# Order of the input projection beside the attention: the first output-gate unit third, six convolution units behind it

## The chip, the cores and the metric

The kernel runs on one core of a Trainium2 chip. The metric is the device time of one execution in microseconds; the time given is the median of several executions. The core's engines work side by side, each through its own list of instructions in order: TensorE (PE in the profile; its weight loads are PEld), VectorE (DVE), ScalarE (ACT), GpSimd (POOL) and SyncE (SP), which issues most DMAs.

## What is computed

One layer of an encoder on a sequence of 1024 tokens of width 1024, in float32. One input projection feeds two groups of heads; what they give is concatenated and projected back, and a SwiGLU network follows.

```python
h = modulate(rms_norm(x, norm_mix_g[l]), sh1, sc1)
proj = h @ w_in[l]
q_a, k_a, v_a, qk_m, v_m, o_m, gates = jnp.split(proj, splits, axis=-1)
y_attn = axial_gqa_attention(q_a, k_a, v_a, q_norm_g[l], k_norm_g[l], tables)
y_mem = bidirectional_mlstm(qk_m, v_m, o_m, gates, conv_w[l], conv_b[l], gate_b[l], mlstm_norm_g[l])
mix = jnp.concatenate([y_attn, y_mem], axis=-1) @ w_out[l]
x = x + g1[:, None, :] * mix
```

The attention has 8 query heads of 64 on 2 key heads, with rotary positions and a softmax over all 1024 keys. The mLSTM has 4 heads of 128 and runs over the sequence in both directions. Its queries and keys, `qk_m`, are 1024 columns that go through a convolution along the sequence, five taps wide, and a silu. Its values `v_m` and its output gates `o_m` are 512 columns each. Input gates and forget gates are 16 columns, of which running sums and maxima are taken.

## The kernel before

Each float32 product is made of three matmuls (`mm3`, lines 310 to 313): both operands are split into a high and a low part, and high by high, high by low and low by high are summed. The normed input lies in SBUF for the whole first half of the program as `hh` and `hl` (8 tiles of 128 rows each).

**The input projection is cut into units.** Those named `q` make two query heads each (`q_unit`). Those named `f` make 128 channels of the convolution's input each (`conv_unit`, line 878): `f` 0 to 3 are the mLSTM's queries, 4 to 7 its keys. Those named `t` make 256 columns, turned so that tokens lie on the partitions (`chunk_unit`, line 936): `t` 0 and 1 are the values of mLSTM heads 0 and 1, and 2 and 3; `t` 2 and 3 the output gates of the same pairs. The list `IN` (lines 47 and 48) is the order in which the units that are left after the program's first stage are gone through.

A conv unit is two halves of 512 tokens, each a sum over 8 steps of three matmuls of 512 columns into a PSUM bank named `acc`. ScalarE copies each half into the tile `xp`. Then a chain of steps follows: five taps on VectorE into the tile `y` (one `TENSOR_SCALAR`, four `SCALAR_TENSOR_TENSOR` of 128x1024), a tanh on ScalarE, a last product on VectorE, and a store to DRAM. A chunk unit is eight parts of 128 tokens, each a sum over 8 steps of three matmuls of 256 columns into a bank named `acct`; ScalarE copies each part into the tile `vstg`, and SP stores it. In the attention's stage `acc` and `acct` share one single bank.

A conv unit begins by waiting for the chain of the conv unit two before it:

```python
yield convs[-2:-1]
```

Weights come in pieces of 256 KB, in the order in which the units use them (`specs`, which is built from `IN` too). A conv unit has two pieces, a chunk unit four. A piece is loaded by SP into the tile `wst`, copied by ScalarE to `whi` and subtracted by GpSimd to `wlo`. There is room for six split pieces. A unit calls for further pieces as it goes through the last of its own (`load_piece`, line 487): a conv unit in its second half, a chunk unit in its last part.

**The order of instructions comes from a planner.** While the program is built, `Clock` keeps an estimated time for every engine. `streams` (line 215) takes the streams in their order of rank: at each step of PE the first stream whose operands are ready by that clock goes on, and the `fills` come last. On the chip every engine goes through the order so found, and waits by semaphores where the estimate was too early.

```python
s = next((s for s in every if s.ready() <= self.t), None)
```

**The attention** is made of three streams of higher rank than the units, over 64 blocks of 128 queries of one head each. `scores` (line 1146) makes the score product `S`; VectorE takes its maximum (`sst`), ScalarE the exponential (`P`, with its sum), VectorE the reciprocal, and GpSimd scales `P`. `turned` (line 1178) transposes `P` on PE into `T`; ScalarE and VectorE copy it out as high and low part (`PT`). `values` (line 1200) multiplies with the values into `av`. Every eight blocks a new head's queries are split (`qs`, ScalarE and GpSimd). Beside them run, on GpSimd and ScalarE, the products for the conditioning (`ada`, `ada_late`, line 1111), and on VectorE and ScalarE the gates' steps (`gate_steps`, line 954; running sums and maxima in the tiles `Fr`, `T`, `mk`, `R`, one step no sooner than 10 us after the other by the planner's clock, line 69). The units are the fill:

```python
ck.streams([Stream(values()), Stream(turned()), Stream(scores())], [un])
ck.streams([un], stop=lambda: convs[-1].done and len(convs) == 8 and not open_sum[0])
```

Units that are left when the attention ends, and when all eight convolutions are done, go on as the fill beside the mLSTM (line 2191), and the output projection's units after them.

Of the kernel before, what the change touches and what calls it, by code (L numbers as in the profile page):

```python
# [43 lines left out]
KB = 5  # L44
AHEAD = 2
NP = NF // 2
IN = ([("q", 2), ("q", 3), ("f", 0), ("f", 4), ("f", 1), ("f", 5), ("t", 2), ("f", 2), ("f", 6),
       ("f", 3), ("f", 7), ("t", 1), ("t", 3)])
MIX = [("o", i) for i in range(16)] + [("m", (i + 8) % 16) for i in range(16)]
FF = [("b", p) for p in range(NB)] + [("v", 0)] + [("s", (p, i)) for p in range(1, NP - 1) for i in range(2)] + [("v", NP - 1)]  # L50
# [199 lines left out]
def layer_kernel(ctx, tc, xT, c, w_ada, vecs, cons, rope, w_f, w_fT, w_t0, w_t, w_o, w_gu, w_d, out):  # L250
# [113 lines left out]
    with tc.manual_schedule():  # L364
# [65 lines left out]
        specs += [t0[0], q1[0], t0[1], t0[2], q1[1], t0[3]]  # L430
        for kind, i in IN + MIX + FF:
            start[kind, i] = len(specs)
# [1656 lines left out]
        def units(order):  # L2089
            for kind, i in order:  # L2090
                yield from {"q": q_unit, "f": conv_unit, "t": chunk_unit, "o": out_unit, "m": out_unit, "b": first_unit, "s": set_unit, "v": pair_unit}[kind](i, start[kind, i])
# [56 lines left out]

        un = Stream(units(IN))
        def ready():  # L2150
            return rope_ok[3].done and logf_ok.done and not open_sum[0]
# [162 lines left out]
```

## Time and profile before

| | us |
|---|---|
| median of 3 runs (1390.51 to 1393.83) | 1393.42 |
| the profiled execution | 1393.51 |
| its span, from the first to the last instruction | 1391.7 |
| first score product | 174.3 |
| end of the attention's last product | 505.1 |

The units' places in the profiled execution, read off the copies of their sums by ScalarE:

| unit | last copy starts at, us |
|---|---|
| f0 | 156.3 |
| f4 | 178.2 |
| f1 | 207.2 |
| f5 | 244.5 |
| t2 | 327.9 |
| f2 | 352.3 |
| f6 | 373.1 |
| f3 | 403.6 |
| f7 | 431.0 |

In rows of the profile a group is written as line, engine, operation, `out<-in` by the tiles' names, and partitions by elements. Line 98 is the helper through which VectorE, ScalarE and GpSimd get all their instructions, so these are told apart by their tiles. Lines 311 to 313 are the three matmuls of `mm3`, line 1158 is `S`, 1190 `T`, 1209 `av`. A row of the timeline begins with its start in us and its length; in brackets stands how long the engine was idle before it, and what ended the idle time. A row of the table by stage gives the stage, its length, the busy time and the number of instructions of each engine, then the granted clock of TensorE as a share of full speed, the DMA engines' share and GB/s.

### The profile page before, as it was taken

To read this page: it belongs to the slowest core of one execution; us is meant where nothing else is said; L and a number is where in the kernel's file an instruction comes from. 1 tells how busy PE (TensorE), PEld (TensorE's weight loads), DVE (VectorE), ACT (ScalarE), POOL (GpSimd) and SP (SyncE) were. 2 spreads that over 40 slices of the span, in tenths; PEclk is the share of its full clock that TensorE was granted. 3 is DMA by queue.
4 is the path that set the end of the run, shared out by engine and by line. 5 is a ranking of instruction groups with operands and counts; after the bars stand their busy time and mean duration, and the time that the engine had idled before them with its cause. 6 is when DMAs were issued, how large, how long until landed. Compare 5 with 4: busy or idle time off the path is not lost.

```text
span 1391.7 us, 19566 instructions
## 1 busy us (share of the span) xinstructions
PE 1289.2 (93%) x6588; PEld 1079.7 (78%) x6596; DVE 1033.3 (74%) x1536; ACT 709.0 (51%) x1335; POOL 706.1 (51%) x584
## 2 busy tenths in 40 slices
PE   7898888899999979989997899999999999979997
PEld 5786677888778978777776788888888887857887
DVE  6936698975789747758689886766676654998866
ACT  6575366778577755454477333332333334344462
POOL 0344677655656525677512265554554545445542
PEclk9999999999999999999999899999999999989999
DMA  9444433233233235663652343233332259733324
GB/s 355 158 129 118 114 103 95 84 99 105 65 108 97 67 131 180 201 225 102 198 187 89 105 138 106 99 107 106 114 114 81 76 178 328 288 79 103 95 64 155
DMA packets 103892, 185.98 MB, mean 134 GB/s; under 512 B 11504, under 2 KB 33136, under 8 KB 103792
## 3 DMA queue, kind: packets, MB, share of 16 engines
q1 hardware_dynamic: 90400, 162.63, 36.8%
q10 hardware_dynamic: 13392, 22.10, 4.2%
q8 instruction: 52, 0.85, 0.2%
q14 instruction: 48, 0.39, 0.1%
HBM read 137.76 MB, written 43.25 MB: 130 GB/s over the span
## 4 chain that ended last, share of the span: by engine, by line
PE 55%; DVE 18%; issue 8%; DMA 6%; ACT 5%; POOL 5%; SPq 1%; DVEq 0%; POOLq 0%; ACTq 0%
PE acc L311 15%; PE acc L312 15%; PE acc L313 15%; DVE sst L98 3%; DVE y L98 2%; DVE PT L98 2%; PE av L1209 2%; DVE x L98 2%; PE T L1190 2%; POOL wlo L98 2%; PE S L1158 1%; SPq L316 1%; DMA x<-in_xT_dram 1%; PE acct L313 1%; DVE s L98 1%
## 5 line engine op out<-in xcount | busy, mean ns | idle before, releaser
L98 POOL TENSOR_TENSOR wlo<-wst,whi 128x512 fp32r<-128x512 f32 (+2 forms) x187 | 264.5, 1420 | 262.3 <-ACT whi L98 236.4
L98 ACT ACTIVATE whi<-wst 128x512 fp32r<-128x512 f32 (+2 forms) x219 | 131.0, 605 | 110.2 <-PE acc L313 34.2
L312 PE MATMUL acc<-x,whi 128*128 128x512 f32 x352 | 138.4, 393 | 5.9 <-DVE x L98 5.9
L98 POOL TENSOR_SCALAR P<-P,sst 128x1024 f32<-128x1024 f32 x64 | 85.1, 1330 | 88.1 <-DVE sst L98 64.3
L98 POOL TENSOR_TENSOR wlo<-wr,whi 128x512 fp32r<-128x512 f32 x56 | 77.4, 1383 | 76.9 <-ACT whi L98 75.5
L311 PE MATMUL acc<-hh,whi 128*128 128x512 f32 x224 | 97.8, 436 | 6.5 <-ACT xp L98 5.3
L311 PE MATMUL acc<-whi,wch 128*128 128x512 f32 x244 | 96.5, 395 | 6.1 <-ACT wch L98 6.1
L313 PE MATMUL acc<-whi,wcl 128*128 128x512 f32 x244 | 96.8, 397 | 2.9 <-DVE wcl L98 2.8
L312 PE MATMUL acc<-wlo,wch 128*128 128x512 f32 x244 | 96.1, 394 | 0.1
L98 ACT ACTIVATE P<-S,sst,colq 128x1024 f32<-128x1024 f32 x64 | 77.2, 1207 | 36.8 <-DVE sst L98 26.9
L98 ACT ACTIVATE whi<-wr 128x512 fp32r<-128x512 f32 x60 | 37.9, 632 | 107.5 <-DVE wr L98 50.1
L98 DVE TENSOR_TENSOR PT<-T,PT 128x512 fp32r<-128x512 f32 x128 | 83.3, 681 | 10.7 <-ACT PT L98 10.5
L312 PE MATMUL acc<-hl,whi 128*128 128x512 f32 x224 | 90.9, 406 | 0.0
L313 PE MATMUL acc<-hh,wlo 128*128 128x512 f32 x224 | 90.8, 405 | 0.0
L98 POOL TENSOR_TENSOR wlo<-s,whi 128x512 fp32r<-128x512 f32 x40 | 54.0, 1352 | 67.5 <-ACT whi L98 67.5
L1190 PE MATMUL T<-ident,P 128*128 128x128 f32 x512 | 72.8, 280 | 15.9 <-DVE PT L98 9.3
L98 DVE TENSOR_TENSOR sg<-acc,sg 128x512 f32<-128x512 f32 x67 | 45.4, 687 | 55.8 <-PE acc L313 55.5
L311 PE MATMUL acct<-whi,hh 128*128 128x256 f32 (+1 forms) x256 | 82.8, 324 | 4.2 <-ACT hh L98 2.8
L98 ACT ACTIVATE PT<-T 128x512 fp32r<-128x512 f32 x128 | 71.8, 596 | 28.5 <-PE T L1190 27.8
L98 DVE TENSOR_REDUCE sst<-S 128x1 f32<-128x1024 f32 x64 | 77.7, 1214 | 11.4 <-PE S L1158 9.9
L312 PEld LDWEIGHTS acc<-x,whi 128*128 128x128 f32 x352 | 66.5, 189 | 21.0 <-DVE x L98 7.3
L98 POOL TENSOR_TENSOR ada<-ada,cond 128x512 f32<-128x512 f32 x48 | 69.2, 1443 | 23.3 <-DMA ada<-in_w_ada_dram 23.2
(478 smaller groups left out, 3859.6 us busy)
## 6 DMA issues: line engine op xcount, KB each, us to landing
wr<-in_w_gu_dram SPq DMA_DIRECT2D x66, 256.0 KB, 2.7
ada<-in_w_ada_dram SPq DMA_DIRECT2D x64, 256.0 KB, 3.2
wd<-in_w_d_dram SPq DMA_DIRECT2D x22, 512.0 KB, 6.4
wst<-in_w_gu_dram SPq DMA_DIRECT2D x34, 256.0 KB, 3.1
wst<-act_d SPq DMA_DIRECT2D x33, 256.0 KB, 4.1
ada<-in_w_ada_dram SPq DMA_DIRECT2D x16, 512.0 KB, 7.1
wst<-in_w_o_dram SPq DMA_DIRECT2D x32, 256.0 KB, 3.9
act_d<-sg ACTq DMA_DIRECT2D x31, 256.0 KB, 2.2
```

Source lines behind the costliest of these rows:

```text
L98: return fn(*args, **kw)
L311: nc.tensor.matmul(acc, w[0], x[0], start=first, stop=False)
L312: nc.tensor.matmul(acc, w[0], x[1], start=False, stop=False)
L313: nc.tensor.matmul(acc, w[1], x[0], start=False, stop=last)
L316: (q or nc.sync).dma_start(dst, src)
L1158: nc.tensor.matmul(sp[:, halves(n)], qs[:, j * P:(j + 1) * P], k2[g][m][:, halves(n)], start=m == 0, stop=m == 1)
L1190: nc.tensor.transpose(tp[:, k], Pt[q][:, (4 * b + k) * P:(4 * b + k + 1) * P], ident)
L1209: nc.tensor.matmul(av, va[:, k, h // 4], PT[it][m][:, k], start=(k, m) == (0, 0), stop=(k, m) == (NJ - 1, 1))
```

## The change

The unit `t` 2 moves from the seventh place of `IN` to the fifth, ahead of `f` 1 and `f` 5. Among the units behind the two of queries it is now third, and the six conv units left follow it without a break. The weight pieces follow, since their list is built from `IN`. The instructions are otherwise the same; their order on every engine is the planner's.

```diff
-IN = ([("q", 2), ("q", 3), ("f", 0), ("f", 4), ("f", 1), ("f", 5), ("t", 2), ("f", 2), ("f", 6),
+IN = ([("q", 2), ("q", 3), ("f", 0), ("f", 4), ("t", 2), ("f", 1), ("f", 5), ("f", 2), ("f", 6),
        ("f", 3), ("f", 7), ("t", 1), ("t", 3)])
```

## The prediction

> **What bounds the kernel now.** I read the page first, then the table by stage, then the chain of work, then the timelines at the places where TensorE stood idle. From the page:
>
> ```profile
> PE 1289.2 (93%) x6588; PEld 1079.7 (78%) x6596; DVE 1033.3 (74%) x1536; ACT 709.0 (51%) x1335; POOL 706.1 (51%) x584
> PE 55%; DVE 18%; issue 8%; DMA 6%; ACT 5%; POOL 5%; SPq 1%; DVEq 0%; POOLq 0%; ACTq 0%
> ```
>
> TensorE (PE) is busy 93% of the span and carries 55% of the chain that ended last, so the program is nearly a list of matmuls, and time is won only where PE idles or runs at a lower clock. The change adds and removes no instruction. It can only move that idle time. The attention runs from its first score product at 174.3 us to 505.1 us, and the table by stage (length, then busy time of PE, PEld, DVE, ACT, POOL; the granted clock follows) cuts it where the fill changes its kind:
>
> ```profile
> 174.30:196.40 22.10, 18.27 (x91) 14.83 (x90) 20.32 (x24) 12.89 (x24) 18.46 (x14) 0.92 0.32 96
> 196.40:244.80 48.40, 42.83 (x235) 36.25 (x234) 42.71 (x59) 31.90 (x63) 34.41 (x22) 0.93 0.33 98
> 244.80:281.30 36.50, 31.87 (x234) 29.17 (x233) 35.69 (x53) 25.60 (x52) 24.13 (x17) 1.00 0.28 84
> 281.30:328.30 47.00, 43.60 (x322) 40.21 (x320) 34.41 (x62) 39.50 (x83) 27.19 (x24) 1.00 0.37 108
> 328.30:432.70 104.40, 98.63 (x558) 82.74 (x559) 79.17 (x131) 69.12 (x136) 60.04 (x50) 0.98 0.30 91
> 432.70:505.10 72.40, 68.71 (x518) 64.10 (x516) 56.85 (x99) 53.74 (x106) 37.38 (x27) 1.00 0.21 62
> ```
>
> PE idles 3.83, 5.57, 4.63, 3.40, 5.77 and 3.69 us in them, 26.9 us in all. DVE is the second engine to fill up: 92%, 88%, 98%, 73%, 76%, 79%.
>
> Which fill runs where, by the same table for one tile's instructions: first acc (conv units, one row), then acct (units of 256 columns, one row), then y (the convolutions' taps; the first number is DVE's, three rows):
>
> ```profile
> 328.30:432.70 104.40, 55.09 (x192) 34.17 (x192) 0.00 (x0) 4.76 (x8) 0.98 0.30 91
> ...
> 281.30:328.30 47.00, 18.76 (x114) 15.93 (x114) 0.00 (x0) 1.93 (x5) 1.00 0.37 108
> ...
> 196.40:244.80 48.40, 12.11 (x8) 2.12 (x2) 0.93 0.33 98
> 244.80:281.30 36.50, 10.03 (x6) 1.06 (x1) 1.00 0.28 84
> 281.30:328.30 47.00, 0.00 (x0) 0.00 (x0) 1.00 0.37 108
> ```
>
> A conv unit is 48 matmuls, so the 192 at 328.3 to 432.7 are exactly the four units f2, f6, f3, f7. The two stretches before that are t2, the unit that moves; those from 174.3 to 244.8 are the end of f4, then f1 and f5. The taps trail their unit: f5's fall into t2's first half, and t2's second half has none.
>
> **The change part by part.** Until f4 is through (its last half runs across the start of the attention) both orders are the same. Then f1, f5, t2 become t2, f1, f5. Loads: t2 has four weight pieces, f1 and f5 two each, all of 256 KB, so the list of pieces keeps its shape, and the same numbers of loads stand on SP's queue, ACT and POOL. SP's stores (8 small ones of t2, one of 512 KB for each conv) swap places among themselves; nothing in the attention reads them, so I put that at nothing. If it were not hidden, one late store would hold a buffer for a few microseconds. From f2 on the order is the old one.
>
> *What goes.* The two largest waits in f1 and f5 (PE's timeline, S is L1158, T is L1190; in brackets the idle time before and who ended it):
>
> ```profile
> 215.21 1.07 PE L1158 MATMUL S<-k,qs 128*128 128x512 f32 x4
> ...
> 219.12 0.66 PE L1190 MATMUL T<-ident,P 128*128 128x128 f32 x4 [2.16 <-POOL P L98]
> ...
> 222.47 1.65 PE L1158 MATMUL S<-k,qs 128*128 128x512 f32 x4
> ...
> 232.86 0.63 PE L1190 MATMUL T<-ident,P 128*128 128x128 f32 x4 [2.95 <-POOL P L98]
> ```
>
> Both wait for POOL to scale a softmax block. After the first the same score products take 1.65 us for 1.07: the clock has dropped. The clock column says how much: 0.93 over 48.4 us is 3.4 us lost, and 0.92 over 22.1 us is 1.8 us. Why POOL was late (POOL's timeline, then DVE's):
>
> ```profile
> 213.40 2.35 POOL L98 TENSOR_TENSOR ada<-ada,cond 128x512 f32<-128x512 f32 x1 [2.04 <-DMA ada<-in_w_ada_dram]
> 215.71 2.25 POOL L98 TENSOR_TENSOR wlo<-wst,whi 128x512 fp32r<-128x512 f32 x1
> 217.96 1.11 POOL L98 TENSOR_SCALAR P<-P,sst 128x1024 f32<-128x1024 f32 x1
> ...
> 226.19 4.51 POOL L98 TENSOR_TENSOR qs<-qd,qs 64x1024 fp32r<-64x1024 f32 x1
> 230.80 1.97 POOL L98 TENSOR_SCALAR P<-P,sst 128x1024 f32<-128x1024 f32 x1
> ...
> 226.21 2.27 DVE L98 TENSOR_TENSOR_SCAN Fr<-mk,Fr 32x1024 f32<-32x1024 f32 x1
> 228.46 3.32 DVE L98 SCALAR_TENSOR_TENSOR y<-xp,vec,y 128x1024 f32<-128x1024 f32 x1
> ```
>
> Three loads meet here: weight splits (wlo), gate scans, and f1's taps; the P step takes 1.97 us instead of 1.11, and a tap 3.32 us. With t2 in this place, f1's taps are not yet there (12.11 us of DVE work in the stretch, of which only f4's last step stays), and no weight split comes until t2's end. The gate scans stay: they are paced on their own.
>
> *The sum*, over 174.3 to 328.3. Before: idle 3.83 + 5.57 + 4.63 + 3.40 = 17.4, clock 1.8 + 3.4 = 5.2, together 22.6 us.
>
> After: (a) to 196.4, f4's taps still meet the first scan: 3.8 + 1.8 = 5.6, as now. (b) t2 took 83 us; some 64 us of it now lie behind 196.4, with scans but no taps. The nearest row is t2's tapless half, 3.40 of 47.0, or 7.2%: 4.6 us, no clock lost. (c) f1 and f5 come in some 67 us. For the first 36.5 us f1's taps meet the remaining gate steps, as f5's do now at 244.8 to 281.3: 4.6 us. (d) The other 30 us resemble the run of four conv units: 5.77 idle and 0.02 of clock in 104.4, 7.5%: 2.3 us. Together 17.1 us. **The gain is 22.6 - 17.1 = 5.5 us.** Bounds: at best t2 also takes away (a)'s clock loss and its 1.9 us wait, and (c) falls to the rate of (d), another 5 us; at worst f1 and f5 keep all of their old waits (5.57 + 3.4 = 9.0 instead of the 6.9 in c and d) and t2 its own 8.0, and nothing is won.
>
> The profiled execution took 1393.51 us with a span of 1391.7, beside a median of 1393.42, so the sum holds for both: 1393.5 - 5.5 = **1388.0 us**. Work that no longer fits into a shorter attention (the rest of t1, all of t3) goes on beside the mLSTM, at no less cost and no more: it is PE work in either place.
>
> The Trainium skill, "TensorE: Matmul & The Clock Gate", "What's actually happening", has the array's clock halve after an idle window of about 3.4 us; by that neither wait above would cost clock, and the estimated gain would be about 2 us. The trace differs: 1.65 us for 1.07 stands behind a wait of 2.16 us.
>
> **The rivals.** *The pile-up travels.* Taps and POOL's steps lengthen each other, and the taps only move. For it: the taps meet P, ada and weight splits wherever they run, and in 281.3 to 328.3, where f5's taps would then fall, ACT is 84% busy (39.50 of 47.0) against 66% where f1's taps lie now (31.90 of 48.4). Against it: the four conv units from 328.3 on have the same taps and lose 7.5% of their time, where f1 and f5 lose 18.5% (5.57 + 3.4 of 48.4). Price: f1 and f5 keep 9.0 us and t2 keeps 8.0, which is what they lose now: 1393 us, give or take 3. The Trainium skill, "SBUF — State Buffer", "Who interferes with whom", speaks for this rival: a VectorE instruction with two SBUF inputs and a GpSimd instruction that reads SBUF hold a shared port in turn, each for its whole length. The 3.32 us tap agrees.
>
> *Slower: a conv unit waits for the chain of the one two before it* (line 879). Six in a row means that f2 cannot start until f1's taps, tanh, product and store are done, and f6 not until f5's are. The chain's and the passes' lengths (evacuations on ACT, last product on DVE):
>
> ```profile
> 244.47 0.60 ACT L98 ACTIVATE xp<-acc 128x512 f32<-128x512 f32 x1
> ...
> 352.27 0.60 ACT L98 ACTIVATE xp<-acc 128x512 f32<-128x512 f32 x1
> ...
> 373.14 0.60 ACT L98 ACTIVATE xp<-acc 128x512 f32<-128x512 f32 x1 [5.72 <-PE acc L313]
> ...
> 279.12 1.86 DVE L98 SCALAR_TENSOR_TENSOR y<-xp,y 128x1024 f32<-128x1024 f32 x1
> ...
> 388.60 1.22 DVE L98 SCALAR_TENSOR_TENSOR y<-xp,y 128x1024 f32<-128x1024 f32 x1
> ```
>
> f5's chain beside the gate steps takes 36.5 us (244.47 to 280.98), f6's only 16.7 (373.14 to 389.82); f6's pass on PE takes 20.9 (352.27 to 373.14), and four passes 104.4, or 26.1 each. Today t2 stands behind f5 and hides the long chain. If f1's and f5's chains both take 36.5 us, f2 and f6 wait 10.4 each, 20.8 us in which PE has no fill. The fill is 55.09 of 104.4 there, 53%, so at most 11.0 us of PE time is lost, plus two drops of the clock like those above (3.4): 1388.0 + 14.4 = 1402; at the least the attention speeds up without fill and half is lost: 1395. I take 1398. It decides from about 10 us of waiting on (5.5 / 0.53). Against it: only f1 will meet the gate steps, f5 just the last of them.
>
> **How the numbers follow.** A measurement of this kernel can tell 0.3%, 4.2 us, from no change. The forecast, 1383 to 1391, has a chance of 0.5; the travelling pile-up 0.3; the hold of the conv chains 0.2. Of the forecast some 0.06 lies within 4.2 us of before, and of the travelling pile-up some 0.02 on either side: faster 0.46, same 0.32, slower 0.22. The range takes the best bound of the sum (1388.0 - 5) and reaches up to the middle of the slower rival: 1382.5 to 1398.5.
>
> **What would show it.** Right: the waits of T for P near 219 and 233 are gone, the clock from 196 to 245 is 1.00, no y instruction starts on DVE between about 203 and 260, and the last tap still comes some 50 us ahead of the attention's end, which has moved from 505.1 to about 499.6. The travelling pile-up would show as waits of T for P or PT of over 2 us between 265 and 330, with a clock under 1.00. The slower rival would show as stretches without any acc matmul near 310 or 335, while PE idles. What would make the prediction wrong besides: the order of all instructions comes from a planner's clock, which may place the gate steps elsewhere once DVE is freer, against other work than I assumed.

## The result, and the profile after

The changed kernel takes 1414.28 us (median; 1413.9 to 1416.05) beside 1393.14 us of the kernel before on the same chip: a ratio of 1.0167, 95% interval 1.0149 to 1.0184. It is 21 us slower, where 5.5 us less had been forecast. The page's first two lines of the profiled execution:

```profile
span 1412.8 us, 19571 instructions
PE 1287.6 (91%) x6596; PEld 1077.8 (76%) x6596; DVE 1044.6 (74%) x1536; ACT 705.9 (50%) x1335; POOL 700.1 (50%) x584
```

PE is busy as long as before (1287.6 us for 1289.2), so the 21 us are idle time. The question is in which stage. The table by stage of the changed kernel, cut at the attention's first and last product and at the mLSTM's last transpose of an output (in the kernel before, the attention's last product ends at 504.2; 505.1 is where the next product starts):

```profile
175.00:513.70 338.70, 310.73 (x2036) 274.05 (x2035) 273.25 (x421) 233.69 (x465) 201.15 (x152) 0.99 0.29 90
513.70:690.70 177.00, 138.03 (x772) 117.07 (x772) 120.84 (x271) 78.50 (x205) 103.65 (x144) 0.90 0.51 164
690.70:1412.80 722.10, 689.81 (x3108) 567.13 (x3106) 535.11 (x667) 294.67 (x501) 324.05 (x238) 0.98 0.40 133
```

The same three stages of the kernel before:

```profile
174.30:504.20 329.90, 303.92 (x1950) 267.31 (x1948) 268.70 (x421) 232.37 (x458) 201.62 (x150) 0.98 0.30 88
504.20:671.40 167.20, 146.68 (x849) 124.81 (x857) 117.24 (x271) 82.11 (x212) 109.26 (x147) 0.98 0.55 182
671.40:1391.70 720.30, 688.90 (x3108) 566.68 (x3106) 531.51 (x667) 295.53 (x501) 326.10 (x240) 0.98 0.40 134
```

The attention is 8.8 us longer (338.7 for 329.9), the mLSTM's stage 9.8 (177.0 for 167.2), the rest 1.8; the start is 0.7 later. But the two stages differ in kind. The attention's extra time is filled: PE idles 28.0 us in it for 26.0 before, and executes 84 more matmuls (the row counts two more, which begin just before the cut and belong to the next stage). In the mLSTM's stage PE executes 77 matmuls fewer and still takes longer: it idles 39.0 us for 20.5.

Those matmuls are fill. The same table for the tile acct (units of 256 columns), attention and mLSTM's stage, of the changed kernel:

```profile
175.00:513.70 338.70, 70.62 (x446) 61.19 (x447) 0.00 (x0) 6.84 (x18) 0.99 0.29 90
513.70:690.70 177.00, 17.62 (x132) 16.17 (x131) 0.00 (x0) 2.31 (x6) 0.90 0.51 164
```

And of the kernel before:

```profile
174.30:504.20 329.90, 60.40 (x360) 50.50 (x360) 0.00 (x0) 5.72 (x15) 0.98 0.30 88
504.20:671.40 167.20, 34.54 (x216) 29.12 (x216) 0.00 (x0) 3.44 (x9) 0.98 0.55 182
```

With three matmuls to a step, and without the two at the cut, the attention took in 148 steps of t units for 120. The 28 steps are worth some 10.1 us of PE time (an estimate: three matmuls 0.12 us apart are 0.36 us). On equal work, then, the attention became some 1.3 us shorter, and the mLSTM's stage, which should have become 10.1 us shorter, lost 19.9. What PE waited for in that stage (who waited for whom; total, times, longest):

```profile
PE U L1910 <- DVE Cs L98: 20.9, 1, 20.9
...
PE acc L311 <- ACT yah L98: 6.2, 1, 6.2
```

One wait of 20.9 us, at 539 to 560. DVE's step Cs, for which it waits, stands in DVE's list behind this (the chain that ended last, in order of time: start, length, what):

```profile
540.24 3.47 DMA ada<-in_w_ada_dram
...
543.80 1.19 DVE ada L98 x2
545.01 2.37 DMA ada<-in_w_ada_dram
...
547.48 0.71 DVE ada L98 x2
548.21 3.00 DMA ada<-in_w_ada_dram
...
558.62 0.70 DVE ada L98 x2
```

Load, product, load, product: the late pieces of the conditioning (ada) come two at a time, a pair each 3.7 us (543.80 to 558.62 in four), and nothing else is put out. The code says why. The mLSTM's first stage lasts until the projection's units are through; then whatever ada pieces are left are gone through alone, because their memory is wanted for the next stage:

```python
ck.streams(mem, [un], stop=lambda: un.wait is None and all(f.done for v in vo_ok for f in v))
while not summed:
    ck.need(*adas[-2:])
    ada_late(64)
```

In the kernel before, t3 runs until 577 us, and all ada pieces are done by then (the last product starts at 557.8). In the changed kernel t3 is through at 537 us. ScalarE's copies of the t units' sums, before and after (shortest, median and longest in ns, then the first and the last start in us):

```profile
L98 ACT ACTIVATE vstg<-acct x32: 369/384/403, 84.1 to 577.5; 128x256 f32<-128x256 f32 x32
L98 ACT ACTIVATE vstg<-acct x32: 367/384/404, 82.5 to 537.3; 128x256 f32<-128x256 f32 x32
```

**Theory A**: the time is lost because the attention used up t3's steps, so the stage ended with ada pieces undone. **Theory B**, the rival: the run of six conv units, or the early place of t2, costs the time.

### The profile page after: what moved, and what is told of

It is laid out like the page before. It is cut to its first block, busy times and chain, and to the rows that moved or that the text cites. A ratio compares the mean times of both kernels' runs of the same rounds, so it can differ in the third digit from the quotient of the medians.

```text
span 1412.8 us, 19571 instructions
## 1 busy us (share of the span) xinstructions
PE 1287.6 (91%) x6596; PEld 1077.8 (76%) x6596; DVE 1044.6 (74%) x1536; ACT 705.9 (50%) x1335; POOL 700.1 (50%) x584
## 4 chain that ended last, share of the span: by engine, by line
PE 55%; DVE 21%; issue 8%; ACT 6%; DMA 5%; POOL 3%; SPq 1%; DVEq 0%; ACTq 0%; POOLq 0%
PE acc L312 15%; PE acc L313 15%; PE acc L311 15%; DVE sst L98 4%; DVE y L98 3%; DVE PT L98 3%; PE av L1209 2%; DVE x L98 2%; PE T L1190 1%; DMA ada<-in_w_ada_dram 1%; PE S L1158 1%; ACT P L98 1%; SPq L316 1%; DVE s L98 1%; PE ni L1994 1%
## 5 line engine op out<-in xcount | busy, mean ns | idle before, releaser
L98 DVE TENSOR_TENSOR PT<-T,PT 128x512 fp32r<-128x512 f32 x128 | 83.8, 681 | 14.4 <-ACT PT L98 14.3
L1209 PE MATMUL av<-PT,va 128*128 128x256 f32 x512 | 73.9, 288 | 11.6 <-DVE PT L98 9.9
```

Source lines behind the costliest of these rows:

```text
L98: return fn(*args, **kw)
L1209: nc.tensor.matmul(av, va[:, k, h // 4], PT[it][m][:, k], start=(k, m) == (0, 0), stop=(k, m) == (NJ - 1, 1))
```

## The experiments

Each run is measured against the kernel before on the same chip.

**1. The changed kernel with the stage held open.** One condition more:

```diff
-ck.streams(mem, [un], stop=lambda: un.wait is None and all(f.done for v in vo_ok for f in v))
+ck.streams(mem, [un], stop=lambda: un.wait is None and all(f.done for v in vo_ok for f in v) and summed)
```

> The changed kernel, with one condition more: the mLSTM's first stage, whose fill is what is left of the projection's units, ends only when the conditioning products (ada) are done too, so that they run beside mLSTM steps instead of by themselves. Theory A (the time is lost because t3 is used up early, the stage ends, and 10 of the 16 ada pieces are then waited for with no other work put out; PE idle for 20.9 us at 539 to 560 in the changed kernel): the idle stretch goes, some 5 us of it come back as unfilled gaps of the mLSTM, 1395 to 1402. Theory B (the run of six conv units, or t2's early place, costs the time inside the attention): 1408 to 1414, since the attention is the same. A third reading, that the 20.9 us would only be passed on to the next stage: 1410 or more, with an idle stretch later.

Measured: 1396.07 us, ratio 1.004 (1.002 to 1.006). Its mLSTM's stage, by the same table:

```profile
512.10:672.50 160.40, 138.40 (x759) 115.35 (x766) 114.74 (x270) 78.47 (x204) 104.41 (x142) 0.96 0.54 178
```

160.4 us for 177.0, with an attention as long as in the changed kernel (337.6 us). Its largest wait in that stage is 2.4 us. One condition on a stage's end brings back 1.3% of the 1.7%: theory A, and not B. What the 0.4% left is made of was not tried.

**2. The old order with its fill used up.** All units left are run at the attention's end:

```diff
-ck.streams([un], stop=lambda: convs[-1].done and len(convs) == 8 and not open_sum[0])
+ck.streams([un])
```

> The kernel before, its old order of units, with one edit: behind the attention all units that are left run at once, so that the mLSTM starts without any fill and its first stage ends at once, with all 16 ada pieces (32 halves, 16 behind the attention) still to come. Theory A: an idle stretch of PE of 25 to 35 us while they come alone, 1415 to 1430. Theory B: the old order has no run of six, so the time stays within 1393 to 1400.

Measured: 1444.86 us, ratio 1.0399 (1.0363 to 1.0436). The wait appears in the old order too:

```profile
PE tr L1882 <- issue: 37.7, 1, 37.7
```

It is longer than expected, but not by the ada pieces. The chain that ended last, inside this wait (which begins at 535.5):

```profile
538.05 4.48 DMA cond<-in_c_dram
...
545.06 2.38 DVE ada L98 x4
547.46 2.55 DMA ada<-in_w_ada_dram
...
570.17 0.71 DVE ada L98 x2
```

The 16 pieces take 25.8 us (545.06 to 570.88), at the low end of the 25 to 35 expected; the 9.5 us ahead of them go mostly to a store and to the conditioning's own input (cond), which here nothing hides either. The time is 15 us above the range: the whole mLSTM then runs without t3, and PE idles 66.7 us up to its end, of which the wait is only 37.7. The direction is A's; the price of a missing fill was set too low.

**3. t2 one place later than before.** No run of six conv units:

```diff
-IN = ([("q", 2), ("q", 3), ("f", 0), ("f", 4), ("f", 1), ("f", 5), ("t", 2), ("f", 2), ("f", 6),
+IN = ([("q", 2), ("q", 3), ("f", 0), ("f", 4), ("f", 1), ("f", 5), ("f", 2), ("t", 2), ("f", 6),
        ("f", 3), ("f", 7), ("t", 1), ("t", 3)])
```

> The order of before with t2 one place later, behind f2: runs of conv units of five and three, none of six, and t2 in the middle of the attention. Theory A: what matters is how much fill the attention takes in, and if this order also takes in more, t3 is used up early here too; by the same idle stretch, 1408 to 1418. Theory B: the shorter runs and the later place put it beside the kernel before, 1388 to 1398.

Measured: 1414.97 us, ratio 1.0192 (1.0151 to 1.0233), the same loss as the changed kernel's. (This kernel has one line less ahead of the code, so its line numbers are one lower.)

```profile
PE U L1909 <- DVE Cs L97: 20.5, 1, 20.5
```

The same wait to half a microsecond, with t2 on the other side of its old place, and again 148 steps of t units in the attention. This speaks most plainly against B: neither the long run of conv units nor the early place is needed for the loss.

**4. The changed order with t3 kept out of the attention.**

```diff
-un = Stream(units(IN))
+un = Stream(units(IN[:-1]))
...
-ck.streams([un], stop=lambda: convs[-1].done and len(convs) == 8 and not open_sum[0])
+ck.streams([un])
+un = Stream(units(IN[-1:]))
```

What is left of t1 is now run before the mLSTM starts; in the trace the attention takes in all of it.

> The changed order, but t3 is kept out of the attention's fill: it starts only with the mLSTM. Theory A: the mLSTM's first stage then has 64 steps of fill (some 23 us of PE time) and lasts until the ada pieces are nearly done; the idle stretch shrinks to under 3 us and the attention loses some fill at its end: 1393 to 1402. Theory B: 1408 to 1414, since the conv units run as in the changed kernel.

Measured: 1391.97 us, ratio 1.0018 (1.0 to 1.0036); in a second series beside the next run 1391.52, ratio 1.0009 (0.9995 to 1.0024), where this stood on record:

> The same kernel as in the earlier run of the changed order with t3 kept back, again, beside the old order with the same edit on one chip: ratio to the kernel before 0.999 to 1.005. By the prediction's sum it would lie 5.5 us under the old order with the edit, by theory B over 4 us above it, and if the attention's idle time only moves, within 3 us of it.

The mLSTM's stage of the first series:

```profile
510.90:668.30 157.40, 141.89 (x824) 120.75 (x833) 119.26 (x271) 79.18 (x207) 103.52 (x143) 0.99 0.57 185
```

157.4 us for 177.0, idle 15.5 for 39.0. With the fill at the place where it is needed, the changed order is level with the kernel before.

**5. The old order with the same edit.**

> The order of before with the edit of the run before (t3 starts only with the mLSTM). In the kernel before the stage's end already finds the ada pieces done, so under theory A the edit changes little: 1386 to 1396 (ratio 0.998 to 1.004). Its ratio against the changed order with the same edit is then what the order alone does to the attention: the prediction's sum has 5.5 us less for the changed order, theory B has over 4 us more, and that the idle time only moves gives under 3 us either way.

Measured: 1398.53 us, ratio 1.0062 (1.0045 to 1.0079), above the range. With this edit the changed order is 7 us ahead of the old one. That looks like the 5.5 us of the prediction, and is not: the attention of this run is as in the kernel before (329.4 us, PE idle 27.3), and the difference lies in the mLSTM's stage (176.2 us for 157.7 in the second series of the changed order). There PE waits twice at the end:

```profile
PE ni L1994 <- DVE num L98: 6.7, 2, 5.9
PE acc L311 <- ACT yah L98: 5.3, 1, 5.3
```

The second is the wait of 6.2 us of the changed kernel: the output projection's second half waits for the mLSTM's last heads, when its first half, the next fill, is used up. Why the old order uses it up here and the changed one does not stays open: this fill starts at 560.4 in the one and at 558.4 in the other. Nor does the attention show a gain for the changed order: it takes 337.0 us there (PE idle 30.3), 7.6 more than in this run, for 8 more steps of fill (some 2.9 us), which the old order runs behind the attention. So this pair does not isolate the order's effect on the attention, as it was meant to.

**6. ada pieces earlier, in the old order.** The attention's blocks may take pieces beyond the 48th:

```diff
-                ada_late()
+                ada_late(64)
```

> The order of before, but the attention may also take ada pieces beyond the 48th (its last blocks take 4 to 6 of them), so that fewer are left for the mLSTM's first stage, which then ends some 18 us earlier by the planner's clock. Theory A: nothing was waited for there in the old order, so only a little is won, from the mLSTM's DVE: 1383 to 1392 (ratio 0.995 to 1.000). Were the ada pieces' number behind the attention of no account, the ratio is 1.000.

Measured: 1388.1 us, ratio 0.9983 (0.997 to 0.9995). It is the best of all here, by less than the 0.3% that can be told from no change.

**7. The same in the changed order**, alone, and with the stage held open.

> The changed order, with ada pieces beyond the 48th allowed in the attention's last blocks and the stage's end as it was. By the planner 8 of the 16 late pieces are then undone when the stage ends, for 12 in the changed kernel and 16 in the old order with its fill used up, whose idle stretches were 20.9 and 37.7 us. Theory A: the stretch shrinks in proportion, to 12 to 16 us, and the time to 1403 to 1409 (ratio 1.009 to 1.014). A stretch of about 20 us all the same would say that something other than the ada pieces is waited for.

Measured: 1409.36 us, ratio 1.0125 (1.0082 to 1.0167). The wait:

```profile
PE U L1910 <- DVE Cs L98: 13.7, 1, 13.7
```

By the planner 8 pieces are undone here, 12 in the changed kernel, 16 in the second experiment: the waits are 13.7 us, 20.9 us and, of the 37.7 there, the 25.8 that the pieces take. That is 1.6 to 1.7 us a piece in all three: the wait follows the number of pieces.

> The changed order with both: ada pieces beyond the 48th in the attention's last blocks, and the mLSTM's first stage held open until they are done. Theory A: the stage is held open for fewer pieces than in the first run, so less of the mLSTM goes without fill: under the 1396 of that run by 2 to 6 us (ratio 0.998 to 1.003). Theory B: no effect on the attention, ratio 1.004 as before.

Measured: 1401.24 us, ratio 1.0078 (1.0061 to 1.0095): worse than the first experiment, against the expectation. The wait for ada is gone here as well, but the one for yah is back:

```profile
PE acc L311 <- ACT yah L98: 6.2, 1, 6.2
```

The stage ends earlier here, so the next fill starts earlier (563.0 for 573.4 in the first experiment), and runs out before the mLSTM's last heads are done. An early start alone does not bring this wait: in the fourth experiment that fill starts at 559.6, and there is none.

**8. Four ada pieces under way** instead of two, in the changed order.

> The changed order, with four ada pieces under way instead of two behind the attention (four buffers for two); nothing else. In the idle stretch of the changed kernel a pair of pieces comes every 3.4 us, its load issued only when the pair before is done. Theory A with the loads' way as the price: the stretch falls to 6 to 12 us, the time to 1398 to 1407. If instead the DVE products or the bytes set the pace (0.7 us and 256 KB each), the stretch stays over 15 us: 1408 to 1414.

Measured: 1406.21 us, ratio 1.012 (1.0088 to 1.0152). The wait:

```profile
PE U L1910 <- DVE Cs L98: 15.9, 1, 15.9
```

And what SP waited for between 535 and 556:

```profile
SPq L316 <- POOL wlo L98: 5.4, 1, 5.4
SPq L316 <- DVE ada L98: 4.2, 3, 2.8
```

The time lies in the first reading's range, the wait (15.9 us) in the second's, so neither held whole; the execution profiled is the slowest of the four (1410.26 us). In the changed kernel SP waits 12.5 us for ada products there, so more buffers do help. But SP's list goes in order, and the last six ada loads, issued from 545.25 on, stood behind a weight load that waited 5.4 us for GpSimd to free its buffer.

## Why the prediction was wrong

The step that failed is the last sentence of the sum: "Work that no longer fits into a shorter attention (the rest of t1, all of t3) goes on beside the mLSTM, at no less cost and no more: it is PE work in either place." It failed in both halves. Work did not move out of the attention but into it, 28 steps. And the place does matter: the steps of t3 were the fill of the mLSTM's first stage, and its end was tied to theirs. Taken away there, they uncovered 20.9 us of ada pieces (experiments 1, 3, 4 and 7). Later in the stage there is a wait of 6.2 us for the mLSTM's last heads besides; it is gone in experiments 1 and 4, but comes in 5 too, where t3 was not taken, so what decides it stays open. I read the attention's stages closely and never asked what ends the stage behind it, though the fill that I moved was what set its end. The forecast and all rivals shared this blind spot, so the range missed too.

*The sum inside the attention* was right in direction over the stretch for which it was made, but not part by part. The changed kernel, cut as the sum was, then to f7's last copy:

```profile
174.30:196.40 22.10, 17.52 (x114) 15.11 (x113) 19.69 (x25) 12.43 (x24) 16.61 (x10) 1.00 0.31 90
196.40:261.00 64.60, 57.52 (x422) 53.16 (x421) 54.07 (x88) 45.74 (x90) 38.10 (x29) 1.00 0.34 104
261.00:328.30 67.30, 64.55 (x380) 54.93 (x379) 54.83 (x83) 52.29 (x109) 41.61 (x34) 1.00 0.24 73
328.30:423.40 95.10, 86.21 (x484) 71.15 (x483) 80.38 (x119) 61.52 (x119) 58.17 (x46) 0.98 0.33 103
```

(a), put at 5.6 us lost, lost 4.6 with no clock lost; (b), put at 4.6, lost 7.1; (c) and (d), put at 6.9 together, lost 2.8. Together 14.4 for the 17.1 expected and 22.6 before: a gain of 8.2 us at 328.3. That the total came near is in part luck, since the errors go both ways. With all but one step of f4's chain gone from it, t2 lost 11% of its stretch, where 7.2% was forecast; with their taps f1 and f5 lost 4.1%, where some 10% was. So the taps alone are not what PE loses time to here. VectorE's work on the gates' tile `Fr` is 11.1 us in t2's stretch and 3.7 in that of f1 and f5; whether that is the reason was not tried. Then the four last conv units, which I had left unchanged, idled 8.9 us in 95.1, where they had idled 5.8 in 104.4 before, and 3.1 us were given back. What was left of it by the end of the attention is the 1.3 us on equal work above; where the rest of the gain went was not worked out.

*Where the 28 steps came in.* Up to f7's last copy both kernels have put in the same fill: the conv units and t2. From there to the attention's end, the table for acct has, in the kernel before:

```profile
431.00:505.10 74.10, 29.03 (x168) 23.76 (x168) 0.00 (x0) 2.67 (x7) 1.00 0.20 62
```

And in the changed one:

```profile
423.40:513.70 90.30, 39.82 (x254) 34.58 (x255) 0.00 (x0) 3.82 (x10) 1.00 0.26 78
```

The same stretches for the score products' line, four matmuls to a block, before:

```profile
431.00:505.10 74.10, 16.35 (x60) 10.25 (x60) 1.00 0.20 62
```

And after:

```profile
423.40:513.70 90.30, 18.55 (x68) 11.63 (x68) 1.00 0.26 78
```

56 steps in 15 blocks before, 84 in 17 after (again without the two matmuls at the cut): 3.7 and 4.9 steps a block. The planner settles into another rhythm of products and fill; in experiment 3 the attention takes in as many steps. PE is as busy in one rhythm as in the other (95% of both stretches), so the rhythm itself costs little; it takes the fill from the next stage. Why it settles so was not tried.

*The rivals.* The travelling pile-up did not come: f1 and f5 lost 2.8 us in 67.3 at a clock of 1.00. By the lock rule of the Trainium skill ("SBUF — State Buffer", "Who interferes with whom") it might have; the rule is not shown wrong by that, since taps of 2.18 us still stand there beside taps of 1.27 (the one at 291.93 begins during GpSimd's ada product of 291.73 to 293.03). The hold of the conv chains did not come either: the longest stretch without fill is 3.3 us near 310 and 6.2 us in the whole attention (361.4 to 367.7), and PE waits nowhere there for more than 2.3 us. The outcome was slower, as this rival has it, by a mechanism that I had not named.

*Of the signs named beforehand*, these held: the clock between 196 and 245 is 1.00 (0.93 before), the waits for P near 219 and 233 are gone, and but for f4's last step at 205.1 no y instruction starts between 203 and 260. These did not: the last one ends 71 us ahead of the attention's end, not some 50, and that end moved to 513.7, not to 499.6.

## What to carry to other kernels

Fill is a stock that the stages share: when an order lets one stage take more of it, look at what the next stage runs on, and at what its end waits for. Where a stage ends on "the fill is used up", list what else must be done by then, and tie the end to all of it; here that one condition was worth 1.3%. And when the busy time stays while the span grows, look for one long wait before explaining many short ones.

## What the runs showed that was not expected

The clock's drop does not follow the length of a wait alone. Before, a wait of 2.16 us was followed by score products of 1.65 us. In the changed kernel a longer one leaves them at full speed (PE's timeline):

```profile
208.22 1.16 PE L1190 MATMUL T<-ident,P 128*128 128x128 f32 x8 [2.27 <-POOL ada L98]
209.76 1.09 PE L1158 MATMUL S<-k,qs 128*128 128x512 f32 x4
```

What decides was not tried. So of the 8.2 us gained up to 328.3, the 5.2 us of clock may be owed as much to where the waits fell as to how long they were.
